# The bidirectional gated scan of a diffusion trunk: units of four tiles, projections by features, and score and output steps for two tiles at once

## The chip, the cores and the metric

The kernel runs on one core of one Trainium2 chip. The metric is device time in microseconds (us) of one execution; lower is better. Shapes are fixed: 2048 latent tokens and 256 context tokens of width 1024, one layer, float32 in and out. Products that must be exact to float32 are made as three TensorE passes over operands that are split into a high and a low part (high x high, high x low, low x high).

## The reference, cut to what matters

```python
def hgrn2_chunk_scan(q, k, v, logf, s0):          # chunks of 64 tokens
    b = jnp.cumsum(logf, axis=3)
    b_ref = b[:, :, :, CHUNK // 2:CHUNK // 2 + 1]
    b_last = b[:, :, :, -1:]
    scores = jnp.einsum('bhnik,bhnjk->bhnij', q * jnp.exp(b - b_ref), k * jnp.exp(b_ref - b))
    o_intra = jnp.einsum('bhnij,bhnjv->bhniv', jnp.where(mask, scores, 0.0), v)
    kv = jnp.einsum('bhnjk,bhnjv->bhnkv', k * jnp.exp(b_last - b), v)
    # S <- exp(b_last) * S + kv over the chunks, s_start = S ahead of each chunk
    o_inter = jnp.einsum('bhnik,bhnkv->bhniv', q * jnp.exp(b), s_start)
    return o_intra + o_inter, s_final

def hgrn2_mixer(h_ctx, h_lat, w_in, lb, g_gain, w_out, need_ctx):
    # w_in (D, 5D): q | f_fwd | f_bwd | i (value) | g (output gate), 8 heads of 128 each
    q = silu(q);  f = lb + (1 - lb) * sigmoid(zf);  logf = log f;  k = 1 - f
    # both directions: scan the context from zero, then the latent tokens from its final state
    o = o_fwd + o_bwd
    return (rmsnorm(o, g_gain) * silu(g)) @ w_out
...
m = silu(c) @ w_ada + b_ada                        # adaLN: shift, scale, gate, twice
lat = lat + g1 * hgrn2_mixer(hc, modulate(rmsnorm(lat), sh1, sc1), ...)
lat = lat + g2 * conv_ffn(modulate(rmsnorm(lat), sh2, sc2), ...)
return rmsnorm(lat, final_g)
```

## The kernel before

Tokens are cut into tiles of 128: tiles -2 and -1 are the context, 0 to 15 the latent tokens. The stages are: adaLN for the first norm (w_ada against the condition, line 209, turned into per-feature A and B, line 224); the scan over heads; the residual stage, which adds the other direction's state (`heads`, line 855), norms, gates, turns (`heads_T`, line 891) and multiplies by the output weight; and the FFN, which the diff doesn't touch.

The scan works in two halves, the groups of `GROUPS`: tiles -2 to 6 and 7 to 15, and in each half through all eight heads, each head in three units of three tiles. The normed, modulated and transposed tokens of a half lie in SBUF as a high and a low part for each unit (`part`, six places). `make_h` prepares a tile: load, square and scale (`normalize`), four transpositions by two into one PSUM buffer (`transpose_mod`, lines 112, 116 and 119), split (lines 80 and 81). The tiles of the second half are prepared inside the last head of the first, between the steps of its units.

A unit (`unit`, line 365) projects with `mm3` (lines 359 to 361: three matmuls for each of eight feature chunks). Gates for the two directions and the query have features as rows and 384 tokens as columns; the value and the output gate have tokens as rows, 256 columns for each tile (`values`, line 413). In the first unit, with two context tiles, query, value and gate of its one latent tile come together with 384 columns and the query is turned; the context values have 256 token columns and are turned. ScalarE takes the sigmoid of the gates (line 405), VectorE their affine `lb + (1 - lb) s` (line 407) and then the factors: running products by `tensor_tensor_scan` (lines 451 and 464), differences and products (`ke`, `qp`, `kd`, `qi`, `km`, `qm`, all three tiles in one instruction); GpSimd makes the small tables `TB` and `TX` and the decays `sd`.

Each tile then has two steps. `part_a` turns `kd` (line 550, copied by ScalarE as `kt`, line 552), makes twelve score matmuls (line 560) and masks them (lines 575 to 577). `part_b` makes `kv` (line 585), `o` from the running state and from the scores (lines 600 and 601), copies both out (lines 602 and 603), updates the state `Sf` on VectorE (line 604) and stores value-sum, `kv`, gate and `qi` in DRAM (`stash`). The steps of one unit are not issued at once; they are a list that the next unit's projections take up by sixths (`fill`) or by chunks (`tick`). TensorE runs what it gets in order, so a step stands between projections, and a wait of a step holds the projections behind it. `ada_rest` (line 631 on) makes the other four adaLN rows with VectorE, one load of 512 KB at a time; `out_weight` multiplies a row block of the output weight by the gate and splits it (lines 653, 80, 81), three for each unit of the last head.

SP issues nearly all loads and stores in order. Weights come through `rawp`, two buffers of 512 KB; at the start 13 buffers take the rows of w_ada and the first head's weights.

The key lines of the order of steps:

```python
order = ((part_a, 0), (part_a, 1), (part_b, 0), (part_a, 2), (part_b, 1), (part_b, 2))
```

Of the kernel before, what the change touches and what calls it, by code (L numbers as in the profile page):

```python
# [38 lines left out]
GROUPS = (  # L39
    ((-2, -1, 0), (1, 2, 3), (4, 5, 6)),  # L40
    ((7, 8, 9), (10, 11, 12), (13, 14, 15)),
)
UN = 384
NSC = 3
NS = 12
# [3 lines left out]
def body(ctx, tc, a, out):  # L49
# [81 lines left out]
    wp = pool_(c1, "wp", 2)  # L131
    hq = pool_(c1, "hq")
    fix = pool_(c1, "fix")


    PLACE = {("h", 0): 0, ("l", 0): 1, ("h", 1): 2, ("l", 1): 3, ("l", 2): 4, ("h", 2): 5}
    parts = {}

    def place(i, shape, dt, name):
        return (hq if i == 5 else hp).tile(shape, dt, name=name, tag=f"place{i}", bufs=1)  # L140

    def part(v, u):

        if (v, u) not in parts:
            parts[v, u] = place(PLACE[v, u], [128, KT, UN], F32R, f"h{v}{u}")
        return parts[v, u]

    def x_tile(p, t, bufs=1, xt=None):
        if xt is None:
            xt = p.tile([128, D], F32, name="xt", tag="xt", bufs=bufs)  # L150
        src, r = (a["x"], t) if t >= 0 else (a["ctx"], t + 2)
        sp.dma_start(xt, src[r * 128:(r + 1) * 128])
        return xt

    def put_split(hm, u, i, ks=slice(None)):

        c = slice(i * 128, (i + 1) * 128)
        split(part("h", u)[:, ks, c], part("l", u)[:, ks, c], hm[:, ks])

    def load_w(h, ty, wh, wl, p=rawp, tag="raw", bufs=2):  # L160
        raw = p.tile([128, D], F32, name="raw", tag=tag, bufs=bufs)
        sp.dma_start(raw, a["w_in"][h, ty])
        split(wh, wl, raw.rearrange("p (k n) -> p k n", k=KT))

    def load_feat(h, **kw):


        feat = []
        for ty in (2, 1):
            wh = wp.tile([128, KT, 128], F32R, name="wh", tag="wh")  # L170
            wl = wp.tile([128, KT, 128], F32R, name="wl", tag="wl")
            load_w(h, ty, wh, wl, **kw)
            feat.append((wh, wl))
        vh = wp.tile([128, KT, 384], F32R, name="vh", tag="vh", bufs=1)
        vl = wp.tile([128, KT, 384], F32R, name="vl", tag="vl", bufs=1)
        load_w(h, 0, vh[:, :, 256:], vl[:, :, 256:], **kw)
        return feat, vh, vl

    def load_vg(h, w, **kw):

        for i in range(2):
            c = slice(i * 128, (i + 1) * 128)
            load_w(h, 3 + i, w[1][:, :, c], w[2][:, :, c], **kw)


    with ExitStack() as c0:
        p0 = pool_(c0, "p0", side="right")
# [5 lines left out]
        staged = [v[:, i] for p, n in ((2, 3), (5, 3), (4, 1))  # L193
                  for v in [place(p, [128, n, D], F32, "x0")] for i in range(n)]

        def early_x(j):

            xt = x_tile(None, first[j], xt=staged[j])
            junk = p0.tile([128, D], F32, name="junk", tag="hm", bufs=3)
            normalize(xt, junk, p0)  # L200

        first = [t for u in GROUPS[0] for t in u]
        for k in range(KT):
            for i in range(2):
                wt = p0.tile([128, D], F32, name="wada", tag="wada", bufs=13)
                (sp if i else act).dma_start(
                    wt, a["w_ada"][k * 128:(k + 1) * 128, i * D:(i + 1) * D])
                for n in range(2):
                    pe.matmul(mps[2 * i + n], silv[:, k, :], wt[:, n * 512:(n + 1) * 512],
                              start=k == 0, stop=k == KT - 1)  # L210
            if 3 <= k < 6:
                early_x(k - 3)
        head0 = load_feat(0, p=p0, tag="wada", bufs=13)
# [12 lines left out]
        hms = [p0.tile([128, KT, 128], F32, name="hm", tag="hm", bufs=3) for _ in range(3)]  # L226
        for g in range(2):
            ks = slice(g * 4, g * 4 + 4)
            for j, hm in enumerate(hms):
                m = 0 if first[j] >= 0 else 1  # L230
                transpose_mod(staged[j], hm, g, p0s, A1[m], B1[m], "tr", 3, (g + j) % 2)
                put_split(hm, 0, j, ks)
        with tc.issue_after(ada_done.ins):
            load_vg(0, head0, p=p0, tag="wada", bufs=13)
        for j in range(3, 7):
            early_x(j)
# [3 lines left out]
        mx = p0.tile([128, 16], F32, name="mx")  # L240
        e2 = p0.tile([128, 2, 16], F32, name="e2")
        eb = p0.tile([128, 32], F32, name="eb")
# [21 lines left out]
    def w_out_part(v, k):  # L264
        if (v, k) not in wos:
            if k < 6:
                keys = [(v, k // 3 * 3 + i) for i in range(3)]
                p = PLACE[v, k // 3]
            else:
                keys = [("h", 6), ("h", 7), ("l", 6)]  # L270
                p = 4
            w = place(p, [128, 3, D], F32R, "wo")
            wos.update({key: w[:, i] for i, key in enumerate(keys)})
        return wos[v, k]


    rest_of_wo = []

    def mixer_scan():
        gp = pool_(c1, "gp", side="right")  # L280
        xp = pool_(c1, "xp", side="right")
# [11 lines left out]
        def mask(name):  # L293
# [1223 lines left out]
```

## Time and profile before

| | us |
|---|---|
| median of three runs (2823.29 to 2826.19) | 2825.01 |
| the profiled execution | 2823.78 |
| its span | 2821.9 |
| first projection of the scan starts | 42.20 |
| last projection of the scan starts | 1283.01 |
| first matmul of the residual stage | 1303.05 |

In the profile's lists PE is TensorE (matmul), PEld its weight load, DVE VectorE, ACT ScalarE, POOL GpSimd, SP SyncE, and L12 is line 12 of the kernel. A timeline row has the start in us, the duration, the engine, the line, the operation, output and inputs by name, the shape and, in brackets, an idle time before it with what ended it; neighbours alike are put in one row with their count. A matmul's duration includes its way through the array, so that matmuls overlap, and the distance from start to start is what one costs in a stream. A row of groups has the count, busy time, mean ns of one, and the idle time before them with what ended it. A row of the waits names who waited for whom: us in total, times, the longest. A row of the windows has the stretch, its length, then the busy time of each engine with the number of instructions, the mean granted clock of TensorE, the share of the DMA engines and GB/s. A row of DMA issues has the count, the size of one and the median us from issue to landing.

### The profile page before, as it was taken

What the parts mean: (1) busy time and instruction counts of PE and PEld (TensorE: products, weight loads), DVE (VectorE), ACT (ScalarE), POOL (GpSimd) and SP (SyncE); (2) the same over time, 40 slices, a digit from 0 to 9 for tenths busy, and PEclk for the clock granted to TensorE, in tenths of its full rate; (3) what the DMA queues carried; (4) which work ended last, traced back from release to release, by engine and by line L of the source; (5) the groups of instructions that cost most, each with busy time, mean ns of one, the idle gap of its engine ahead of it and who ended that gap; (6) DMA issues with size and microseconds to landing.
All of it is one profiled execution on the core that took longest, in us unless ns stands there. A gap on an engine that the chain in (4) does not pass through costs nothing. (4 is left out here: it accounts for less than half of the span.)

```text
span 2821.9 us, 47353 instructions
## 1 busy us (share of the span) xinstructions
PE 2771.7 (98%) x18064; PEld 2443.6 (87%) x18064; DVE 2061.7 (73%) x3619; ACT 1092.2 (39%) x2165; POOL 616.0 (22%) x1019
## 2 busy tenths in 40 slices
PE   8999999999999999998999899999999999999998
PEld 4999999999999999997887688888888888877887
DVE  5766666676766766677997788877877787576887
ACT  5322322354222222233555444444444444333343
POOL 2112222121221211211111443333344331000001
PEclk9999999999999999999999999999999999999999
DMA  6222222222322322236788422226322223987663
GB/s 239 69 84 80 87 84 87 71 93 71 94 86 69 114 72 74 67 96 220 290 308 308 160 90 90 90 69 236 137 82 90 90 88 104 316 296 251 195 197 123
DMA packets 202635, 385.74 MB, mean 137 GB/s; under 512 B 26660, under 2 KB 117796, under 8 KB 197160
## 3 DMA queue, kind: packets, MB, share of 16 engines
q1 hardware_dynamic: 199672, 374.46, 39.2%
q10 hardware_dynamic: 2736, 8.26, 0.8%
q8 instruction: 142, 2.33, 0.3%
q14 instruction: 85, 0.70, 0.1%
HBM read 280.65 MB, written 101.99 MB: 136 GB/s over the span
## 5 line engine op out<-in xcount | busy, mean ns | idle before, releaser
L359 PE MATMUL z<-vh,hh 128*128 128x256 f32 (+1 forms) x1024 | 300.2, 293 | 0.0
L361 PE MATMUL z<-vh,hl 128*128 128x256 f32 (+1 forms) x1024 | 293.2, 286 | 0.0
L360 PE MATMUL z<-vl,hh 128*128 128x256 f32 (+1 forms) x1024 | 293.0, 286 | 0.0
L359 PE MATMUL z<-hh,wh 128*128 128x384 f32 x768 | 264.8, 345 | 3.0 <-ACT hh L80 3.0
L360 PE MATMUL z<-hl,wh 128*128 128x384 f32 x768 | 258.1, 336 | 0.5 <-DVE hl L81 0.5
L361 PE MATMUL z<-hh,wl 128*128 128x384 f32 x768 | 258.2, 336 | 0.0
L1347 PE MATMUL y<-wd,mh 128*128 128x512 f32 x600 | 234.5, 391 | 2.4 <-ACT X L1382 2.1
L1349 PE MATMUL y<-wd,ml 128*128 128x512 f32 x600 | 234.6, 391 | 1.1 <-DVE ml L81 1.1
L1348 PE MATMUL y<-wd,mh 128*128 128x512 f32 x600 | 234.0, 390 | 0.0
L359 PEld LDWEIGHTS z<-vh,hh 128*128 128x128 f32 x1024 | 196.0, 191 | 0.1
L360 PEld LDWEIGHTS z<-vl,hh 128*128 128x128 f32 x1024 | 195.8, 191 | 0.0
L487 POOL COPY TX<-S 128x3 f32<-128x3 f32 x48 | 31.1, 648 | 753.7 <-DVE S L451 753.7
L361 PEld LDWEIGHTS z<-vh,hl 128*128 128x128 f32 x1024 | 195.5, 191 | 0.0
L81 DVE TENSOR_TENSOR w<-raw,w 128x512 fp32r<-128x512 f32 x180 | 142.0, 793 | 45.6 <-ACT w L80 43.6
L80 ACT ACTIVATE w<-raw 128x512 fp32r<-128x512 f32 x180 | 111.9, 629 | 144.1 <-PE zd L752 78.5
L81 DVE TENSOR_TENSOR w<-s,w 128x512 fp32r<-128x512 f32 x126 | 122.1, 974 | 49.6 <-ACT w L80 48.8
L359 PEld LDWEIGHTS z<-hh,wh 128*128 128x128 f32 x768 | 144.8, 189 | 8.8 <-ACT hh L80 3.6
L427 DVE TENSOR_TENSOR st<-z,st 128x128 f32<-128x128 f32 x127 | 36.4, 287 | 153.3 <-ACT st L426 153.1
L360 PEld LDWEIGHTS z<-hl,wh 128*128 128x128 f32 x768 | 145.2, 189 | 0.8 <-DVE hl L81 0.7
L361 PEld LDWEIGHTS z<-hh,wl 128*128 128x128 f32 x768 | 144.8, 189 | 0.0
L422 ACT ACTIVATE v<-z 128x128 f32<-128x128 f32 x128 | 35.4, 277 | 270.6 <-PE z L361 270.5
L749 PE MATMUL zc<-rT,w 128*128 128x512 f32 x352 | 137.1, 389 | 3.1 <-DVE uv L1234 3.0
(327 smaller groups left out, 7840.1 us busy)
## 6 DMA issues: line engine op xcount, KB each, us to landing
raw<-in_w_up_dram SPq DMA_DIRECT2D x88, 512.0 KB, 3.5
raw<-in_w_in_dram SPq DMA_DIRECT2D x80, 512.0 KB, 3.6
lr<-m SPq DMA_DIRECT2D x49, 512.0 KB, 5.8
m<-r SPq DMA_DIRECT2D x66, 256.0 KB, 3.6
raw<-in_w_ada_dram SPq DMA_DIRECT2D x32, 512.0 KB, 4.7
stash<-st SPq DMA_DIRECT2D x125, 128.0 KB, 1.8
kq<-stash SPq DMA_DIRECT2D x15, 1024.0 KB, 7.2
og<-stash SPq DMA_DIRECT2D x15, 1024.0 KB, 6.2
```

What stands on the lines that cost most here:

```text
L80: act.activation(h, src, AF.Copy)
L81: dve.tensor_tensor(l, src, h.bitcast(F32), OP.subtract)
L359: pe.matmul(o, sh[:, k], mh[:, k], start=k == 0, stop=False)
L360: pe.matmul(o, sh[:, k], ml[:, k], start=False, stop=False)
L361: pe.matmul(o, sl[:, k], mh[:, k], start=False, stop=k == KT - 1)
L422: act.activation(v[:, s], z[:, 0:128], AF.Copy)
L427: dve.tensor_tensor(st[:, 1], z[:, 128:256], st[:, 1], OP.mult)
L487: pool.tensor_copy(TX[:, 0, :, 0], tot[:, 0, :, 1])
L749: pe.matmul(o, w[:, 0, k], r[:, :, 0, k], start=start and k == 0, stop=False, skip_group_check=True)
L1347: pe.matmul(z, lh, rh, start=start, stop=False, skip_group_check=True)
L1348: pe.matmul(z, lh, rl, start=False, stop=False, skip_group_check=True)
L1349: pe.matmul(z, ll, rh, start=False, stop=stop, skip_group_check=True)
```

## The change

- The scan has units of four tiles, 512 tokens (`UT`, `NS` = 16). A half is two units, tiles 0 to 7 and 8 to 15; the context tiles are handled apart, in the first half, ahead of the units of each head: gates, factors, values and `context_state`.
- All five projections have features as rows and 512 tokens as columns (`project`, `acc`); the context's have 256. Tokens lie in blocks of one unit and four feature chunks, high and low together (`tok`).
- Values are copied out as `vt`, turned by four transpositions into one PSUM tile and copied as `v` (`values`, `turn`). The output gate stays by features (`swish`, `keep_gate`); in the residual stage it is multiplied after the transposition, and the norm's factor by one VectorE product for four heads and ScalarE copies for the other four.
- The affine of the gates moves from VectorE to ScalarE (`gates`).
- `scores` makes turnings, scores and masks of two tiles at once, `outputs` the `kv` and `o` of two tiles and both updates of `Sf`. Within a pair, the second tile multiplies its scores first and the state last.
- Steps are asked for by a clock of projection triples (`at`, `tick`).
- Weights of one type lie in one tile of four (`wp`). Tiles 8 to 15 are prepared during heads 2 to 5 of the first half, put into DRAM (`tok_d`) and loaded as four blocks of 2048 KB ahead of the second half.
- At the start, w_ada lies in the later token blocks; tiles -2 to 4 are loaded and normed there with the scaling on ScalarE. Output weights 0 to 3 are prepared in the last head, 4 to 7 after it. The split of the residual stage reads SBUF; `pl` (line 1020) takes three places instead of four.

```diff
+        def acc(z, w, rs):
+
+            for k in range(KT):
+                r = rs[k // 4]
+                h, l = r[:, :, 0, k % 4], r[:, :, 1, k % 4]
+                pe.matmul(z, w[:, 0, k], h, start=k == 0, stop=False, skip_group_check=True)
+                pe.matmul(z, w[:, 0, k], l, start=False, stop=False, skip_group_check=True)
+                pe.matmul(z, w[:, 1, k], h, start=False, stop=k == KT - 1, skip_group_check=True)
+                tick()
+        def gates(d, h, u, z):
...
+            act.activation(F, zv[:, :, 31::-1] if d else zv, AF.Sigmoid)
+            act.activation(F, F, AF.Identity, bias=lb[:, j:j + 1], scale=oml[:, j:j + 1])
+        def values(z, n):
+
+            vt = gp.tile([128, UT, 128], F32, name="vt", tag="vt", bufs=1)
+            act.activation(vt[:, 0:n], z, AF.Copy)
+            v = gp.tile([128, UT, 128], F32, name="v", tag="v", bufs=2)
+            def turn():
+                tr = ps.tile([128, n, 128], F32, name="tr", tag="tr")
+                for i in range(n):
+                    pe.transpose(tr[:, i], vt[:, i], ident)
+                act.activation(v[:, 0:n], tr, AF.Copy)
...
+            def outputs(p, v):
...
+                for d in (1, 0):
+                    for i in range(2):
+                        pe.matmul(kv[:, d, i], kt[:, i, d], v[:, s0 + i], start=True, stop=True)
+                for i in range(2):
+                    s = s0 + i
+                    inner = qi[:, 1, 4 * s:4 * s + 4]
+                    pairs = [(inner, Sf[:, h]), (at_[:, i], v[:, s])]
+                    for n, (l, r) in enumerate(pairs[::-1] if i else pairs):
+                        pe.matmul(o[:, i], l, r, start=n == 0, stop=n == 1)
+                    dve.scalar_tensor_tensor(Sf[:, h], Sf[:, h], sd[:, 1, s:s + 1], kv[:, 1, i],
+                                             OP.mult, OP.add)
...
+            gate(0)
+            query(0, (20, 28))
+            gate(1)
+            query(1, (22, 28))
+            value(0, (6, 10))
+            out_gate(0)
+            if g == 1 and h == NH - 1:
+                for k in range(4):
+                    at(clock[0] + 2 * k, lambda k=k: out_weight(k))
+            value(1, (10, 16))
+            out_gate(1)
...
+                if g == 0 and 2 <= h < 6:
+                    for n in range(2):
+                        for i, f in enumerate(make_tok(HT + 2 * (h - 2) + n)):
+                            at(clock[0] + 8 + 44 * n + 8 * i, f)
+                if g == 1 and h == 0:
+                    for u in range(2):
+                        for kh in range(2):
+                            del tok[u, kh]
+                            sp.dma_start(block(u, kh).bitcast(F32), tok_d[u][kh])
...
-            for h in range(NH):
-                dve.scalar_tensor_tensor(og[:, h, 0], og[:, h, 0], rs[:, h:h + 1],
-                                         og[:, h, 1], OP.mult, OP.mult)
+            o = og[:, 0:4, 0]
+            dve.tensor_tensor(o, o, rs[:, 0:4, None].to_broadcast([128, 4, 128]), OP.mult)
+            for h in range(4, NH):
+                act.activation(og[:, h, 0], og[:, h, 0], AF.Copy, scale=rs[:, h:h + 1])
...
-                split(gh[:, hs], gl[:, hs], tp)
+                g = og[:, hs, 1]
+                dve.tensor_tensor(g, tp, g, OP.mult)
+                split(gh[:, hs], gl[:, hs], g)
```

659 lines of the change are left out of this document (311 added, 348 removed).

## The prediction, made before the change was run

> **What bounds the kernel now.** I read the page first: the share of each engine.
>
> ```profile
> PE 2771.7 (98%) x18064; PEld 2443.6 (87%) x18064; DVE 2061.7 (73%) x3619; ACT 1092.2 (39%) x2165; POOL 616.0 (22%) x1019
> ```
>
> TensorE is busy for 98% of the span, so a gain must come out of TensorE's own sequence, and what the change leaves to other engines counts only where it makes TensorE stand still. Next, the windows: the scan, which is nearly all that the diff touches, from its first projection to its last.
>
> ```profile
> 42.00:1283.00 1241.00, 1229.34 (x11033) 1184.19 (x11034) 840.73 (x1858) 395.21 (x1061) 242.55 (x592) 1.00 0.26 82
> ```
>
> After the span of 1241.00 us come the busy times of PE (1229.34), its weight loads, DVE (840.73, 68%), ACT (395.21, 32%) and POOL; the granted clock is 1.00. TensorE is idle for 12 us in all. "Busy" overlaps here, so a matmul's price is its distance to the next one's start. Grouping by line and shape gives the counts, the timeline the distances.
>
> ```profile
> L359 PE MATMUL z<-vh,hh 128*128 128x256 f32 x960 | 278.1, 290 | 0.0
> L359 PE MATMUL z<-hh,wh 128*128 128x384 f32 x768 | 264.8, 345 | 3.0 <-ACT hh L80 3.0
> L359 PE MATMUL z<-hh,vh 128*128 128x384 f32 x320 | 111.2, 347 | 0.0
> ```
>
> ```profile
> 799.75 0.28 PE L360 MATMUL z<-vl,hh 128*128 128x256 f32 x1
> ...
> 804.20 0.28 PE L361 MATMUL z<-vh,hl 128*128 128x256 f32 x1
> 804.32 0.34 PE L359 MATMUL z<-hh,wh 128*128 128x384 f32 x1
> ...
> 808.31 0.34 PE L361 MATMUL z<-hh,wl 128*128 128x384 f32 x1
> 808.49 0.38 PE L550 MATMUL tr<-ident,kd 128*128 128x128 f32 x2
> 808.80 0.32 PE L560 MATMUL sc<-qm,km 128*32 128x64 f32 x8
> 808.93 0.36 PE L560 MATMUL sc<-qp,ke 128*32 128x32 f32 x16
> 809.22 0.44 PE L359 MATMUL z<-hh,wh 128*128 128x384 f32 x1
> 809.50 0.33 PE L360 MATMUL z<-hl,wh 128*128 128x384 f32 x1
> ```
>
> From 799.75 to 804.20 lie 37 steps of 256 columns: 0.1203 us each. From 804.32 to 808.31 lie 23 of 384: 0.1735. The 512-column matmuls of the FFN give the third width, 42 steps in 9.52 us, 0.2267 each:
>
> ```profile
> 1990.11 0.39 PE L749 MATMUL zc<-rT,w 128*128 128x512 f32 x1
> ...
> 1999.63 0.39 PE L749 MATMUL zd<-rB,w 128*128 128x512 f32 x1
> ```
>
> 256 columns more cost 0.1064 us (2.4 columns per ns), and each matmul has a fixed part of about 13.6 ns whatever its width.
>
> **Term 1, wider projections.** Each group above has its like on L360 and L361. Two smaller forms come from the code: in the first unit of eight heads the one latent tile takes 8 x 8 triples of 384 columns, and the context values 8 x 8 triples of 256. That makes 3 x (768 + 320 + 64) = 3456 matmuls of 384 and 3 x (960 + 64) = 3072 of 256, in all 599.6 + 369.6 = 969.2 us. After the change 16 head passes x 2 units x 5 types x 24 = 3840 have 512 columns, and 8 heads x 3 types x 24 = 576 (context) have 256: 870.5 + 69.3 = 939.8 us. The columns stay the same; only 2112 fixed parts go: -29.4 us. Bounds -28 to -30, since all three distances are measured.
>
> The Trainium skill, in "TensorE: Matmul & The Clock Gate", section "Wait — 56ns, not 53.3ns?", has a start-to-start of N / 2.4 GHz plus about 2.5 ns; by that 2112 fewer matmuls would be worth an estimated 5 us. The rows above disagree, with 13 to 14 ns at each of three widths, and they decide the forecast.
>
> **Term 2, values turned afterwards.** Values are now projected by features, so each latent tile needs one transposition per head (128), with 16 for the context as before; the 8 of a query part go. Net 120. A pair of fp32 transpositions took 808.80 - 808.49 = 0.31 us with the change-over, 0.155 each; without one, the kv group below gives 0.44 / 4 = 0.11 for a pass of the same size. They now come four in a row, so the price is 0.11: +13.2 us (upper end +18.6). The ACT copies that go with them (two of 512 columns per unit, 0.6 us) lie on an engine that is 32% busy.
>
> ```profile
> 1266.60 0.61 PE L585 MATMUL kv<-v,kt 128*128 128x128 f32 x4
> 1267.04 0.39 PE L600 MATMUL o<-Sf,qi 128*128 128x128 f32 x2
> ```
>
> **Term 3, scores of two tiles at once.** One tile's group (two turnings, twelve score matmuls) runs from 808.49 to 809.22, 0.73 us, and delays the projection behind it by 809.50 - 809.22 - 0.1735 = 0.11: 0.84 us. What two in a row cost shows at the end of the scan, where the second tile's scores followed at once:
>
> ```profile
> 1283.13 0.38 PE L550 MATMUL tr<-ident,kd 128*128 128x128 f32 x2
> 1283.44 0.32 PE L560 MATMUL sc<-qm,km 128*32 128x64 f32 x8
> ...
> 1284.15 0.49 PE L600 MATMUL o<-Sf,qi 128*128 128x128 f32 x2
> ```
>
> 1.02 us for one pair of turnings and two sets of scores; with the second pair of turnings (0.22) and the 0.11 behind it 1.35, against 2 x 0.84 = 1.68. 64 pairs x 0.33 = -21 us; lower bound half of that, if part of the change-over stays. The number of kv, o and score matmuls does not change. Terms 1 to 3: -37.2 us.
>
> **Term 4, the hand-over inside a pair.** Outputs now run two tiles in one group: the second tile's o<-Sf needs the Sf that DVE updates after the first tile's o<-Sf has read it. In the built order only one to eight projection matmuls stand between, and TensorE takes its work in order, so everything behind waits too. The end of the scan shows this chain without cover:
>
> ```profile
> 1287.76 1.22 DVE L967 TENSOR_TENSOR wo<-raw,wo 128x1024 fp32r<-128x1024 f32 x1
> ...
> 1288.24 0.39 PE L600 MATMUL o<-Sf,qi 128*128 128x128 f32 x2
> ...
> 1289.03 0.35 DVE L604 SCALAR_TENSOR_TENSOR Sf<-Sf,sd,kv 128x128 f32<-128x128 f32 x1
> ...
> 1289.43 0.71 PE L585 MATMUL kv<-v,kt 128*128 128x128 f32 x4 [0.57 <-DVE Sf L604]
> ```
>
> From the read of Sf to the next use: 0.39 + 0.35 and two hops of some 0.06, about 0.85 us with DVE free (here 1.19, as an operation of 1.22 us held DVE until 1288.98). The cover is three o matmuls (0.22 each, that of the read among them) and one projection (0.23), 0.9 us. So the wait is nought with DVE free, and up to about 1.2 us if a long operation has just begun. DVE is 68% busy, mostly with operations of 0.3 to 1.3 us; I take 0.1 us per pair, +6 us, between 0 and +20 (a quarter of the worst, 64 x 1.25 = 80).
>
> **Term 5, the start.** Before, three x tiles were prepared ahead of the adaLN copies; now squares and scaled copies of tiles 1 to 4 also stand ahead of them in ACT's order, and the raw buffers are two instead of thirteen.
>
> ```profile
> 35.73 0.59 ACT L216 ACTIVATE m<-mps 2x512 f32<-2x512 f32 x1 [0.27 <-PE mps L209]
> ...
> 40.48 1.67 ACT L80 ACTIVATE hh<-hm 128x512 fp32r<-128x512 f32 x3
> ...
> 42.20 0.44 PE L359 MATMUL z<-hh,wh 128*128 128x384 f32 x1 [0.71 <-ACT hh L80]
> ...
> 45.83 1.11 ACT L100 ACTIVATE junk<-x 128x1024 f32<-128x1024 f32 x1
> ```
>
> A tile costs ACT about 1.11 (square) + 1.1 (scaled copy, by the same size), so four cost some 8.9 us: last m copy at about 45 instead of 36.3, first projection near 51. Only three context projections (72 x 0.12 = 8.7 us) can then run, and the first unit of 512 needs tiles 0 to 3 split, which go through one hm buffer and one turning buffer at some 5 us each: first latent projection near 73 to 74. Before, stalls of some 7 us lay there too (waits for hh, x, hm). I take +12, between +5 (the tiles overlap) and +16.
>
> **Term 6, the middle.** Today the second half's tiles are prepared inside one head, and TensorE waits there:
>
> ```profile
> PE tp L112 <- ACT kt L552: 1.7, 2, 1.1
> PE tr L550 <- DVE hm L119: 1.4, 1, 1.4
> PE kv L585 <- DVE Sf L593: 1.1, 1, 1.1
> PE kv L585 <- DVE Sf L604: 0.4, 1, 0.4
> ```
>
> These 4.6 us, of a window 595 to 665, go, since the change spreads that work over four heads: -4.6. In their place four blocks come back from DRAM, as transfers of the size of
>
> ```profile
> rT<-rhs0T SPq DMA_DIRECT2D x4, 2048.0 KB, 10.7
> ```
>
> The first two are freed by the output gate of the first half's last unit of tiles 0 to 3, two projections (10.9 us) and their step work ahead of need, some 14 to 16 us with the half projection between the two blocks; behind them on SP nothing is due but the next weights, whose loads stand ahead. Hidden, at a risk of 0 to +5. What hides it are those two projections: without them it costs 10.7.
>
> **Term 7, the end of the scan.** Four output weights are prepared after the last head, the last two loads waiting for raw buffers, and the first stash loads queue behind them on SP.
>
> ```profile
> 1290.42 1.95 PE L869 MATMUL oi<-Sb,kq 128*128 128x128 f32 x16
> 1295.88 0.46 PE L869 MATMUL oi<-Sb,kq 128*128 128x128 f32 x2 [3.50 <-DVE rs L76]
> ...
> 1303.05 0.77 PE L906 MATMUL y<-wo,ghl 128*128 128x512 f32 x1
> ```
>
> From the last projection's end (1283.13) to the first residual matmul pass 19.9 us now, 8 of them idle. Each weight takes DVE 1.28 + 1.22 us, so the raw buffer for the last is free some 5.5 us after the end and the stash of tile 15 lands near +12 instead of before it; I reckon 23.5 us to the residual and 3.4 us less work within: +7, between +3 and +10.
>
> **Edits at nothing.** The gate's affine goes from DVE to ACT; per-unit factors keep their element counts, with a third fewer instructions. Scores are asked for 20 or more ticks of three matmuls (13 us) after the query, against about 8 us of DVE work behind it. In the residual stage DVE loses eight products per tile and gains three wider ones, ACT gains four copies; the stage is TensorE's:
>
> ```profile
> 1400.00:1450.00 50.00, 50.00 (x283) 43.14 (x282) 44.71 (x112) 26.77 (x61) 7.93 (x7) 1.00 0.80 298
> ```
>
> 0, within 3 either way; if TensorE's cover were gone there, DVE's 44.71 of 50 us would be next. The FFN is untouched.
>
> **Sum.** -29.4 + 13.2 - 21 + 6 + 12 - 4.6 + 7 = -16.8 us, against the profiled execution's 2823.78 (span 2821.9 and 1.9 around it): 2807. The median of the runs is 1.2 us above that execution, so 2808.
>
> **Rivals.** (a) Slower: the hand-over in a pair decides. Without it the sum is -22.8; above 0.45 us per pair (64 x 0.45 = 28.8) the kernel is slower by more than 5.6. For it: 1.19 us in the row above with DVE occupied, and a DVE that is 68% busy. Against it: the cover of 0.9 us, and DVE's many short operations. At 1 us per pair: +64 - 22.8 = +41, about 2866. (b) No change that can be measured: the start and the end cost their upper bounds (+7 more), turnings too (+5), and the pairs save half (+10): 2830, or about 2824 with two of the three. (c) A larger gain: the start costs +5, the hand-over and the risks nothing: -30, 2795. (d) The fixed part of a matmul doesn't go: if the weight load sets the distance and grows with a 512-column neighbour, term 1 is -5 and the sum +7.6: 2833. Against it: weight loads are 1184 of 1241 us busy beside the narrow matmuls, and the 512-column row already includes them. This is the case that the skill's 2.5 ns would give.
>
> **How the numbers follow.** A difference of 0.2%, 5.6 us, is about what the measurement can tell from none. The forecast has 0.48, its own range 2796 to 2820; (c) 0.17; (b) 0.16, half of it inside 0.2% and the rest above or below; (a) 0.16; (d) 0.03. So faster 0.65, same 0.15, slower 0.20. The range 2792 to 2838 leaves out the worst of (a) and the best of (c).
>
> **What would show it.** The page after should have 3840 projections of 512 columns about 0.227 us apart and no wait near the start of the second half; the first of them near 73; o<-Sf waits in the list of waits (0.1 us a pair; more speaks for (a)); between the last projection and the first residual matmul about 23 us. I am wrong if the projections stand further apart, if the waits for Sf, at or kd sum to over 25 us, or if the blocks come late.

## The result, and the profile after

The changed kernel takes 2856.1 us in the median (2853.37 to 2858.47, 4 runs) against 2824.47 us before (2823.29 to 2826.19, 4 runs): 1.0111 times as long, 95% interval 1.0094 to 1.0129. It is slower by 32 us where 17 us less was forecast, and lies outside the range. The profiled execution of the changed kernel took 2855.47 us, its span is 2853.8.

First the share of the engines in the changed kernel, from the page:

```profile
PE 2764.3 (97%) x16072; PEld 2277.4 (80%) x16072; DVE 1988.9 (70%) x2900; ACT 1158.9 (41%) x1910; POOL 574.6 (20%) x884
```

TensorE is busy for 7.4 us less, and the span grew by 31.9: the time went into standing still and into slower work, not into more work. To find where, I cut both spans at the same four events: the first projection, the last projection, the first and the last residual matmul. Windows of the kernel before between these events (stretch, length, busy time of PE, PEld, DVE, ACT, POOL with counts, granted clock, share of DMA, GB/s):

```profile
42.20:1283.00 1240.80, 1229.34 (x11033) 1184.19 (x11034) 840.53 (x1858) 395.01 (x1060) 242.55 (x592) 1.00 0.26 81
1283.00:1303.00 20.00, 12.94 (x145) 11.09 (x144) 14.96 (x41) 8.44 (x20) 1.76 (x2) 0.86 0.82 306
1303.00:1531.00 228.00, 227.24 (x1231) 193.90 (x1231) 196.67 (x482) 117.80 (x261) 35.81 (x30) 1.00 0.77 287
```

And of the changed kernel:

```profile
52.60:1284.80 1232.20, 1209.07 (x9114) 1010.82 (x9113) 770.65 (x1216) 428.45 (x729) 196.47 (x452) 0.99 0.30 95
1284.80:1315.00 30.20, 15.89 (x73) 14.06 (x72) 20.45 (x38) 9.36 (x20) 2.08 (x3) 0.66 0.77 275
1315.00:1568.00 253.00, 236.59 (x1231) 196.20 (x1232) 196.44 (x409) 140.91 (x323) 33.82 (x30) 0.98 0.74 260
```

| stage | before | after | difference | forecast |
|---|---|---|---|---|
| to the first projection | 42.2 | 52.6 | +10.5 | +8.9 |
| first to last projection | 1240.8 | 1232.0 | -8.8 | -29.3 |
| last projection to first residual matmul | 20.0 | 30.5 | +10.4 | +3.6 |
| residual stage | 228.5 | 253.0 | +24.5 | 0 |
| the rest (FFN) | 1290.4 | 1285.7 | -4.7 | 0 |

(The exact events lie some tenths beside the edges of the windows; the sum of the differences is 31.9. The scan's forecast is -16.2 for terms 1 and 2, -21 for term 3, +6, -4.6, the 3.1 of the start that lie behind the first projection, and 3.4 of term 7's +7: the prediction reckons 23.5 us, +3.6, for the end itself, and 3.4 us of work that moves out of it.) The residual stage, where nothing was expected, misses by 24.5 us, the scan by 20.5 and the end by 6.8.

**The projections are what was forecast.** Groups and a stretch of the timeline of the changed kernel:

```profile
L332 PE MATMUL z<-tok,w 128*128 128x512 f32 x1280 | 516.7, 404 | 0.1
L332 PE MATMUL z<-cxt,w 128*128 128x256 f32 x192 | 57.0, 297 | 0.0
```

```profile
1167.17 0.39 PE L334 MATMUL z<-tok,w 128*128 128x512 f32 x1
...
1179.86 0.39 PE L333 MATMUL z<-tok,w 128*128 128x512 f32 x1
```

3 x 1280 of 512 columns and 3 x 192 of 256, and 56 steps in 12.69 us: 0.2266 us each.

**Where TensorE stands.** The list of TensorE's waits in the changed kernel (us in total, times, longest):

```profile
PE o L543 <- DVE Sf L544: 12.4, 14, 3.8
PE y L917 <- ACT ghl L77: 10.0, 7, 3.3
PE oi L877 <- DMA kq<-stash: 9.3, 2, 4.8
PE mt L213 <- ACT m L209: 8.1, 1, 8.1
...
PE tr L476 <- ACT vt L470: 2.5, 3, 1.6
```

The first is the hand-over of term 4, the second the residual stage, the third the end of the scan, the fourth the start.

To see all of the scan's loss I added up, over every matmul from the first to the last projection, the distance to the next start, and set against it a clean pace for each kind (0.2267, 0.1735 and 0.1203 us for 512, 384 and 256 columns, 0.112 for a pass of kv or o, 0.109 for a transposition, 0.013 for a score, 0.428 for an adaLN row). What is above the clean pace counts as a wait if it lies over 0.1 us above the median for the same kinds of matmul ahead, here and behind:

| us | before | after | difference |
|---|---|---|---|
| clean pace of all matmuls | 1180.7 | 1165.0 | -15.7 |
| change-overs at scores | 41.7 | 21.0 | -20.7 |
| change-overs at kv and o | 1.6 | 5.2 | +3.6 |
| projections and turnings above their pace | 1.9 | 8.8 | +6.9 |
| waits | 15.1 | 32.2 | +17.1 |

The first row is a count of matmuls times their pace, so its -15.7 (-16.2 forecast) says that the forecast counted rightly; that the pace holds is shown by the 56 steps above. The second row is measured: -20.7, where term 3 has -21. The gain was all there; the waits and the slower pace took 27.6 us of it, of which 4.5 had been forecast.

**One long wait of the hand-over** in the changed kernel's timeline:

```profile
979.93 1.22 DVE L78 TENSOR_TENSOR w<-raw,w 128x1024 fp32r<-128x1024 f32 x1
...
981.14 0.39 PE L543 MATMUL o<-Sf,qi 128*128 128x128 f32 x2
981.17 5.55 SPq L586 DMA_DIRECT2D raw<-in_w_ada_dram  x2
...
985.08 1.28 DVE L590 SCALAR_TENSOR_TENSOR acc<-raw,sil,acc 128x1024 f32<-128x1024 f32 x1 [3.60 <-DMA raw<-in_w_ada_dram]
986.28 0.34 DVE L544 SCALAR_TENSOR_TENSOR Sf<-Sf,sd,kv 128x128 f32<-128x128 f32 x1
986.67 0.80 PE L543 MATMUL o<-Sf,qi 128*128 128x128 f32 x2 [3.78 <-DVE Sf L544]
```

The state could have been updated at 981.6. But VectorE's next instruction was an adaLN row product that stood 3.60 us for a 512-KB load. Only behind it came the update, and TensorE stood 3.78 us. The load was late because it, too, had waited for VectorE: weights and adaLN rows share the two buffers of `rawp`, and the load was issued at 981.17, when VectorE's split of a weight (L78 at 979.93, the last reader of a `raw` buffer) had just ended. The loads behind VectorE's waits of 3.62 us (until 696.47) and 3.53 us (until 1126.86) were issued right behind such a split as well; no run gives the rows a buffer of their own. The two passes behind the wait took 0.80 us instead of 0.39, and a window around the place shows a lower clock:

```profile
980.00:990.00 10.00, 6.22 (x29) 5.06 (x28) 4.22 (x8) 1.36 (x3) 0.00 (x0) 0.83 0.40 122
```

The granted clock is 0.83 there. The Trainium skill, "TensorE: Matmul & The Clock Gate", section "HAM oscillation — how this bites in real kernels", asks for no idle of TensorE above about 3.4 us; this row, with a wait of 3.78 us, agrees. Shorter waits were not safe here, though: behind two of 2.46 and 1.55 us in the residual stage (until 1376.65 and 1381.04) the clock of the window 1380:1385 was 0.73.

**The residual stage.** Two neighbouring tiles in the changed kernel's timeline: the split of the first ends and the next load into its buffer is issued; the second is turned, multiplied by its gate, split and used (the rows of other work are left out):

```profile
1412.77 0.69 DVE L78 TENSOR_TENSOR ghl<-og,ghl 128x512 fp32r<-128x512 f32 x1
...
1413.52 0.32 SPq L858 DMA_DIRECT2D og<-stash  x1
...
1417.47 1.04 PE L906 MATMUL tp<-ident,og 128*128 128x128 f32 x8
...
1420.44 1.28 DVE L881 TENSOR_TENSOR og<-og,oi 128x512 f32<-128x512 f32 x2 [1.54 <-DMA og<-stash]
...
1423.44 0.68 DVE L908 TENSOR_TENSOR og<-tp,og 128x512 f32<-128x512 f32 x1
...
1424.15 0.63 ACT L77 ACTIVATE ghl<-og 128x512 fp32r<-128x512 f32 x1 [1.73 <-DVE og L908]
...
1426.41 0.48 PE L917 MATMUL y<-wo,ghl 128*128 128x512 f32 x1
```

The transposition ends near 1418.5, yet its product with the gate (L908) starts only at 1423.44: ahead of it in VectorE's order stand the add of the next tile (L881), which waits 1.54 us for its load, and the work behind that add. That load could be issued only when the tile before had freed the buffer. The product alone doesn't free it: its result is written back into the buffer and the split reads it there. The split's last operation (L78) ends at 1413.46, the load is issued at 1413.52; all 14 loads behind the first two are issued within 0.1 us of that operation's end, 1.4 to 3.8 us after the product's. VectorE's waits for this load, of the kernel before (its residual stage) and of the changed one:

```profile
DVE og L873 <- DMA og<-stash: 1.4, 2, 1.1
```

```profile
DVE og L881 <- DMA og<-stash: 17.0, 8, 3.7
```

In this tile TensorE still had other passes until 1426.4. Its waits in the stage, before (1304 to 1520 us) and after (1316 to 1550):

```profile
PE y L908 <- DVE ghl L81: 0.3, 1, 0.3
```

```profile
PE y L917 <- ACT ghl L77: 9.3, 6, 3.3
PE tp L109 <- DVE rs L73: 2.8, 3, 1.8
PE tp L109 <- DVE xn L929: 2.8, 2, 2.5
PE y L919 <- DVE ghl L78: 0.8, 2, 0.6
```

That is 15.7 us instead of 0.3. In the windows above TensorE is also busy for 9.4 us more with the same matmuls (236.59 against 227.24), at a granted clock of 0.98 instead of 1.00; together that is about the 24.5.

So the theory for the residual stage: the gate product and the split that reads it come after the transposition and so keep the tile's buffer (two in all) longer, the next load lands late, VectorE stands before the add, and the product behind it is late too: a loop through a buffer, a queue and an in-order engine. The rival: one VectorE operation more on the way from transposition to matmul.

**The end of the scan** in the changed kernel:

```profile
1290.29 0.80 PE L543 MATMUL o<-Sf,qi 128*128 128x128 f32 x2 [3.72 <-DVE Sf L544]
...
1294.49 0.33 SPq L858 DMA_DIRECT2D kq<-stash  x1
...
1300.57 3.60 PE L877 MATMUL oi<-Sb,kq 128*128 128x128 f32 x16 [4.79 <-DMA kq<-stash]
```

The stash load of the last tile is issued 9.9 us after the last projection (1284.62; in the kernel before 2.5 us ahead of it, at 1280.52). The 16 passes that wait for it start 16.0 us after the last projection and take 3.60 us where they took 1.95 before.

**The start** in the changed kernel:

```profile
41.76 1.15 ACT L100 ACTIVATE x<-x,rs 128x1024 f32<-128x1024 f32 x1 [0.91 <-POOL rs L74]
42.81 2.00 ACT L209 ACTIVATE m<-mps 2x512 f32<-2x512 f32 x4
...
52.65 0.56 PE L332 MATMUL z<-cxt,w 128*128 128x256 f32 x1
...
74.83 0.78 PE L332 MATMUL z<-tok,w 128*128 128x512 f32 x1
```

The adaLN copies end at 44.8 (45 forecast), behind the last scaled copy; the first projection is at 52.65 (51) and the first latent one at 74.83 (73 to 74).

### The profile page after: what moved, and what is told of

Same layout as the page of the kernel before. It is cut to its first block, busy times and chain, and to the rows that moved or that the text cites. A ratio compares the mean times of both kernels' runs of the same rounds, so it can differ in the third digit from the quotient of the medians.

```text
span 2853.8 us, 41978 instructions
## 1 busy us (share of the span) xinstructions
PE 2764.3 (97%) x16072; PEld 2277.4 (80%) x16072; DVE 1988.9 (70%) x2900; ACT 1158.9 (41%) x1910; POOL 574.6 (20%) x884
## 4 chain that ended last, share of the span: by engine, by line
PE 71%; DMA 11%; DVE 11%; ACT 3%; issue 2%; POOL 2%; SPq 0%; DVEq 0%; POOLq 0%; ACTq 0%
PE z L332 9%; PE z L334 9%; PE z L333 9%; PE y L1359 3%; PE y L1357 3%; PE y L1358 3%; PE zd L759 3%; PE zc L759 3%; PE zc L761 3%; PE zd L761 3%; PE zd L762 3%; PE zc L762 3%; PE za L761 3%; PE za L762 3%; PE za L759 3%
## 5 line engine op out<-in xcount | busy, mean ns | idle before, releaser
L332 PE MATMUL z<-tok,w 128*128 128x512 f32 x1280 | 516.7, 404 | 0.1
L333 PE MATMUL z<-tok,w 128*128 128x512 f32 x1280 | 505.1, 395 | 0.0
L334 PE MATMUL z<-tok,w 128*128 128x512 f32 x1280 | 501.8, 392 | 0.3 <-DVE w L78 0.3
L78 DVE TENSOR_TENSOR w<-raw,w 128x512 fp32r<-128x512 f32 (+1 forms) x260 | 239.3, 924 | 88.3 <-ACT w L77 86.1
L332 PEld LDWEIGHTS z<-tok,w 128*128 128x128 f32 x1280 | 241.3, 189 | 49.7 <-issue 2.6
L334 PEld LDWEIGHTS z<-tok,w 128*128 128x128 f32 x1280 | 240.9, 188 | 50.0 <-DVE w L78 0.6
L333 PEld LDWEIGHTS z<-tok,w 128*128 128x128 f32 x1280 | 241.6, 189 | 44.3
L77 ACT ACTIVATE w<-raw 128x512 fp32r<-128x512 f32 (+1 forms) x260 | 195.9, 760 | 177.4 <-PE zd L762 77.4
L78 DVE TENSOR_TENSOR w<-s,w 128x512 fp32r<-128x512 f32 x126 | 121.2, 967 | 53.9 <-ACT w L77 53.1
L759 PE MATMUL zc<-rT,w 128*128 128x512 f32 x352 | 137.1, 390 | 1.2 <-DVE uv L1244 1.0
L762 PE MATMUL zc<-rT,w 128*128 128x512 f32 x352 | 137.0, 389 | 0.0
L761 PE MATMUL zc<-rT,w 128*128 128x512 f32 x352 | 136.9, 389 | 0.0
L1357 PEld LDWEIGHTS y<-wd,mh 128*128 128x128 f32 x600 | 113.3, 189 | 27.2 <-ACT X L1392 3.7
L385 DVE TENSOR_TENSOR_SCAN S<-F,d 128x528 f32<-128x528 f32 (+1 forms) x80 | 91.5, 1144 | 62.2 <-ACT F L368 62.1
L77 ACT ACTIVATE w<-s 128x512 fp32r<-128x512 f32 x126 | 78.2, 627 | 138.8 <-POOL s L815 81.8
L1359 PEld LDWEIGHTS y<-wd,ml 128*128 128x128 f32 x600 | 113.2, 189 | 25.3 <-DVE ml L78 1.4
L1358 PEld LDWEIGHTS y<-wd,mh 128*128 128x128 f32 x600 | 113.3, 189 | 23.4
L759 PE MATMUL za<-rB,w 128*128 128x512 f32 x336 | 130.7, 389 | 0.0
L761 PE MATMUL za<-rB,w 128*128 128x512 f32 x336 | 130.7, 389 | 0.0
```

What stands on the lines that cost most here:

```text
L77: act.activation(h, src, AF.Copy)
L78: dve.tensor_tensor(l, src, h.bitcast(F32), OP.subtract)
L332: pe.matmul(z, w[:, 0, k], h, start=k == 0, stop=False, skip_group_check=True)
L333: pe.matmul(z, w[:, 0, k], l, start=False, stop=False, skip_group_check=True)
L334: pe.matmul(z, w[:, 1, k], h, start=False, stop=k == KT - 1, skip_group_check=True)
L385: dve.tensor_tensor_scan(flat(S[:, d]), flat(F[:, d]), flat(d1[:, 0:ns]), 0.0, OP.mult, OP.max)
```

## The experiments

All times are medians beside the kernel before on the same chip. That kernel took 2824.5 us beside the changed one and 2822.9, 2823.2 and 2825.2 us beside the others, so a gain is given as the difference of what each lies above it; the change lies 31.6 us above. Three edits first, each aimed at one stage, and with the first of them one run that leaves work out and one that makes the stage's edit alone.

**Two loads for value-sum and gate.**

```diff
-    ogs2 = qp.tile([128, 2, NH, 2, 128], ...)
+    ogs2 = qp.tile([128, 2, 2, NH, 128], ...)
...
                 gts[t - 3] = load_stash(1, t - 3)
+            if t > 1:
+                gates2[t - 2] = load_stash(2, t - 2)
```

> The changed kernel with one thing other: value-sum and output gate of a tile come by two loads into two buffers, the gate's asked for a period later, so that the next value-sum no longer waits until the gate has been multiplied. Theory A (the residual stage lost its 24.5 us because a tile's buffer is held until the late gate product, so that the next load lands late and VectorE, in order, stands before the add): VectorE's wait for that load falls from 17.0 us to under 4, TensorE's wait for the split (9.3 us) nearly goes, and the stage from first to last residual matmul goes from 253.0 to 228 to 236 us; total 2832 to 2840. Rival B (the one VectorE product more between transposition and matmul is the cost, wherever the load stands): the stage stays above 246 us and the total within 6 us of 2856.

Measured: 2829.07 us, ratio 1.002 (1.0011 to 1.003), 6.1 us above the kernel before and so 25.5 less than the change. The residual stage of this kernel as a window, and VectorE's wait for the load:

```profile
1313.40:1542.00 228.60, 227.63 (x1231) 193.67 (x1232) 196.06 (x411) 139.49 (x321) 34.58 (x30) 1.00 0.82 289
```

```profile
DVE og L886 <- DMA og<-stash: 0.6, 1, 0.6
```

The stage is 228.7 us long instead of 253.0, the wait 0.6 us instead of 17.0, with every operation of the changed stage still in its place. Theory A holds; the operation by itself isn't the cost. (The total is 3 us under the expected band.) The two loads are also half as large, but they land hardly sooner: 5.9 us after their issue in the median, against 6.4.

**No gate product.** Here the product with the output gate is left out.

```diff
-                g = og[:, hs, 1]
-                dve.tensor_tensor(g, tp, g, OP.mult)
-                split(gh[:, hs], gl[:, hs], g)
+                split(gh[:, hs], gl[:, hs], tp)
```

> The changed kernel without the product with the output gate: the split reads the transposition's PSUM directly as before the change; the gate is stored and loaded but left out of the result. Both theories expect the stage back near 228 to 232 us (total 2830 to 2836), A since the buffer is free at the transposition, B since the chain is one operation shorter. If it stays above 240 us, neither holds and the split of the norm's factor between VectorE and ScalarE or the loads themselves are the cause.

Measured: 2824.74 us (ratio 1.0007, 0.9998 to 1.0017; 5 us under the expected band), the stage 227.0 us. Value-sum and gate come by one load here, as in the change, so the size of the load alone isn't the cause either: the split reads the turned tile directly, the buffer is free at the transposition again, and VectorE's wait for the load is gone from its list. What the product costs in the stage when the loads are apart is 228.7 - 227.0 = 1.7 us; the medians of the two runs lie 4.3 us apart. No run separates the product from the split's reading of the buffer.

**The same edit alone, on the kernel before.** The other direction:

```diff
-            for h in range(NH):
-                dve.scalar_tensor_tensor(og[:, h, 0], og[:, h, 0], rs[:, h:h + 1],
-                                         og[:, h, 1], OP.mult, OP.mult)
+            o = og[:, 0:4, 0]
+            dve.tensor_tensor(o, o, rs[:, 0:4, None].to_broadcast([128, 4, 128]), OP.mult)
+            for h in range(4, NH):
+                act.activation(og[:, h, 0], og[:, h, 0], AF.Copy, scale=rs[:, h:h + 1])
...
-                split(gh[:, hs], gl[:, hs], tp)
+                g = og[:, hs, 1]
+                dve.tensor_tensor(g, tp, g, OP.mult)
+                split(gh[:, hs], gl[:, hs], g)
```

> The kernel before with only the residual stage's edit: the norm's factor by one VectorE product for four heads and four ScalarE copies, and the output gate multiplied after the transposition; the gate is stored there by tokens, so the product takes it unturned. Theory A (the held buffer makes the stage long, by itself and without any of the scan's edits): the stage from first to last residual matmul goes from 228.5 to 245 to 255 us, VectorE waits over 12 us for the load of the value-sum, total 2840 to 2850. Rival: the stage stays under 235 us here, and the loss needs something else of the change, such as the stash written in smaller pieces or the end of the scan coming later.

Measured: 2848.55 us, ratio 1.0083 (1.0067 to 1.0099). Window of the stage and VectorE's wait in this kernel:

```profile
1303.00:1558.00 255.00, 237.14 (x1233) 196.98 (x1232) 195.39 (x409) 139.69 (x321) 33.43 (x30) 0.97 0.74 259
```

```profile
DVE og L873 <- DMA og<-stash: 19.7, 10, 4.2
```

The stage goes from 228.5 to 255.2 us, 0.2 over the band. It is the edit of the residual stage, alone, whatever the scan does before it: 23.4 us in the total.

**Outputs of a pair in two steps.**

```diff
-                for i in range(2):
+                def tile_out(i):
...
+                tile_out(0)
+                at(clock[0] + 2, second)        # second: tile_out(1), copies and stores
```

> The changed kernel with the outputs of a pair in two steps, the second tile two projection triples (1.36 us) behind the first; scores stay in pairs. Theory C (TensorE stands in the scan because the second tile's use of the state follows the first within 0.9 us): the waits of o for Sf up to the last projection fall from 8.7 us to under 3 us, the last projection starts 6 to 10 us earlier (1275 to 1279 us instead of 1284.6). Rival D (the waits come from VectorE standing before an operation that waits for a transfer, so 1.36 us more are too few for the long ones): the short ones of some 0.3 us in the first half go (2.6 us), the long ones of the second half (up to 3.8 us) stay, and the last projection starts 2 to 5 us earlier, the rest of the change being switches between steps and projections.

Measured: 2841.11 us, ratio 1.0065 (1.005 to 1.008), 13.5 us less than the change. The last projection starts at 1275.1, and of the waits for the state there is left:

```profile
PE o L543 <- DVE Sf L544: 3.7, 3, 1.9
```

That is in the whole kernel, and none of it before the last projection: the long waits of o went too, against rival D. Time alone isn't the reason, as this run's timeline shows at the place of the long wait:

```profile
978.14 0.35 DVE L544 SCALAR_TENSOR_TENSOR Sf<-Sf,sd,kv 128x128 f32<-128x128 f32 x1 [0.65 <-PE o L543]
...
981.01 1.28 DVE L595 SCALAR_TENSOR_TENSOR acc<-raw,sil,acc 128x1024 f32<-128x1024 f32 x1 [2.52 <-DMA raw<-in_w_ada_dram]
```

VectorE still stands for the load, but the first tile's update now comes ahead of that product in its order, and only the second tile's, which is needed a group later, behind it. A part of the wait comes back there: kv waits 1.47 us for ScalarE's copy at 983.02. By the accounting above the scan's waits behind the first 150 us fell from 19.2 to 11.1 us and the change-overs at kv and o from 5.2 to 2.0. In the profiled executions 9.6 us lie in the scan and some 3 behind it.

**Norming of tiles 1 to 4 behind the adaLN copies.**

```diff
-        for t in range(1, 5):
-            early_x(t)
+        with tc.issue_after(ada_done.ins):
+            for t in range(1, 5):
+                early_x(t)
```

> The changed kernel with the loading and norming of x tiles 1 to 4 asked for only behind the adaLN copies, as the diff left it to the scheduler before. Theory E (ScalarE's squares and scaled copies ahead of the adaLN copies delay the whole scan): the first projection starts at 43 to 46 us instead of 52.7, but the tiles are needed soon after, so the first latent projection only 2 to 6 us earlier than 74.8; total 2 to 6 us less. Rival F (the four tiles' preparation sets the first latent projection, in whatever order): it starts at 74 to 78 us and the total is the same within 2 us.

Measured: 2849.03 us, ratio 1.0092 (1.0076 to 1.0109), 5.5 us less than the change. First projection and first latent projection of this kernel:

```profile
40.65 0.39 PE L333 MATMUL z<-cxt,w 128*128 128x256 f32 x1 [0.26 <-ACT cxt L77]
```

```profile
69.33 0.77 PE L333 MATMUL z<-tok,w 128*128 128x512 f32 x1
```

The first projection is 12 us earlier (a little earlier than expected), the first latent one 5.5. E holds, and F doesn't: the first latent projection is at 69.33, not at 74 to 78. That the four tiles' preparation sets what is left is likely, since TensorE's waits until then are those of their transpositions and of the context (14.4 us in all, the longest 4.1), but wasn't tried.

**All three together.**

> The two loads, the outputs in two steps and the later norming of tiles 1 to 4 together, on the changed kernel. Theory G (the three losses lie in different stages and add): 2856 - 27 - 15 - 7 gives 2807, with a range of 2803 to 2814: first latent projection near 69, last projection near 1269, stage 228 to 230 us; clearly faster than the kernel before (2823). Rival H (the shares overlap or the clock takes them back): above 2818.

Measured: 2815.33 us (2812.57 to 2819.78, 9 runs), ratio 0.9971 (0.9962 to 0.9981): faster than the kernel before. It lies 7.9 us below the kernel before, so the three edits give 39.5 us of the 44.5 that their sum makes; the last projection starts at 1271.6 (1269 expected), the stage takes 229.3. The total lies between what G expects (up to 2814) and what H expects (above 2818); 5 us are not accounted for.

**Scores of a pair in two steps**, on top of all three.

```diff
-                kts[p] = turned(kd, 2 * p, 2)
...
+                tile_scores(0)
+                if h == 0 and t0 == 0:
+                    second()
+                else:
+                    at(clock[0] + 2, second)    # second: tile_scores(1), copy, masks
```

> As the kernel with all three, but turnings and scores of a pair in two steps, the second tile's two triples behind the first's (in the first head at once), and one copy and one masking for the pair as before. Theory K (term 3: each group pays its change-over, 0.33 us): 63 pairs make the last projection 18 to 22 us later and the total 15 to 22 us longer than with all three. Rival L (the change-over is hidden or was paid already by the row of steps): less than 8 us longer.

Measured: 2840.66 us, ratio 1.006 (1.0047 to 1.0074), 25.3 more than with all three; the last projection at 1295.6 instead of 1271.6. The scan as a window, with all three edits and then with scores in two steps besides:

```profile
41.50:1271.60 1230.10, 1205.96 (x9112) 1010.91 (x9113) 773.15 (x1223) 435.23 (x741) 204.58 (x456) 0.99 0.31 95
```

```profile
41.30:1295.60 1254.30, 1227.17 (x9111) 1015.81 (x9112) 776.66 (x1225) 433.19 (x741) 206.93 (x456) 0.99 0.30 93
```

As many matmuls, 21.2 us more busy time and a scan that is 24.2 us longer: change-overs at scores rise from 20.7 to 41.3 us by the accounting, 0.33 us for each of 63 pairs. Term 3 is shown, slightly above its band.

**Early last outputs, and two buffers for the last weights.** Two attempts at the end of the scan, on top of all three.

```diff
-            value(1, (10, 16))
+            value(1, (4, 8) if g == 1 and h == NH - 1 else (10, 16))
```

> As the kernel with all three, and in the last head of all the outputs of the last unit are asked for 4 and 8 triples behind the value instead of 10 and 16, so that most of them lie under the last projection. Theory I (the end of the scan is long because the last outputs and their stores come only then, and the first stash load waits for their buffers): from the last projection to the first residual matmul 22 to 26 us instead of 29 to 30, total 3 to 7 us less than with all three. Rival J (VectorE's four output weights and the weight loads ahead on SP set the end): the same within 2 us.

Measured: 2813.08 us (2812.39 to 2816.19, 5 runs), the end 25.6 us long instead of 28.7. The end moved as theory I says, but the total by 2.3 us, within the spread of both kernels.

```diff
-            raw = rawp.tile([128, D], F32, name="raw", tag="raw")
+            p, tag = {6: (xp, "hm"), 7: (xp, "stg")}.get(k, (rawp, "raw"))
+            raw = p.tile([128, D], F32, name="raw", tag=tag)
```

> As the kernel with the early outputs, and the last two output weights (6 and 7) are loaded into two buffers of their own that are idle in the second half, so that they don't wait for the buffers of weights 4 and 5 and the first stash load isn't queued behind them on SP. Theory I expects no more than 2 us against the early outputs alone; J expects the stash load of tile 15 issued some 3 to 6 us earlier and 3 to 6 us less in total.

Measured: 2811.74 us (2810.29 to 2818.77, 5 runs), ratio to the kernel before 0.9964 (0.9951 to 0.9977), the end 24.2 us. The load of tile 15 is issued at 1278.04 instead of 1281.10, 5.8 us after the last projection, as J expects, but the total falls by 1.3 us, as I does, again within the spread; so neither is shown. TensorE waits for the load all the same, and its clock falls meanwhile:

```profile
1272.20:1296.40 24.20, 11.69 (x58) 10.70 (x57) 15.42 (x28) 7.35 (x18) 2.94 (x3) 0.65 0.81 288
```

What holds that load besides the weights isn't settled; ahead of it on SP stand the stores of the last output gate.

**Values turned two triples later**, on top of the last.

```diff
-                at(clock[0] + 2, turn)
+                at(clock[0] + 4, turn)
...
-            value(1, (4, 8) if g == 1 and h == NH - 1 else (10, 16))
+            value(1, (6, 9) if g == 1 and h == NH - 1 else (10, 16))
```

> As the kernel with the early outputs and the two buffers for the last weights, and the transpositions of the values are asked for four triples behind the projection instead of two (the last outputs at 6 and 9). Theory M (what is left of the scan's idle, some 5 us before the turning of values, comes from ScalarE's copy not being done 1.36 us after the projection): the waits of the turning for the copy go from 4 us to under 1 us and the total is 2 to 5 us less than 2812. Rival: the copy stands behind a split that waits for a weight's transfer, longer than 2.7 us; then less than 1 us is gained.

Measured: 2816.81 us (2812.07 to 2819.7, 6 runs), ratio 0.997 (0.9958 to 0.9982): no gain. The waits of this kernel:

```profile
PE kv L543 <- ACT sk L559: 6.4, 3, 2.7
...
PE o L549 <- DVE Sf L550: 6.0, 3, 3.7
...
PE tr L482 <- ACT vt L476: 1.1, 2, 0.7
```

The turning's wait went from 4.1 to 1.1 us and came back one step on: kv's wait for ScalarE's copies from 3.4 to 6.4. The state's went from 1.5 to 6.0, but 5.0 of it lies behind the last projection, where this run also moves the outputs. It is ScalarE and VectorE that are late at such places, and a later step only meets them elsewhere, which fits the rival. In the run before this one ScalarE stood 4.69 and 4.29 us for a weight's load (until 752.88 and 966.03) just ahead of the two copies that the turning waited for. In this one kv's longest wait, until 979.73, goes back by ScalarE's copy and the update of the state to an adaLN product that stood 3.13 us for its load. A run without these loads wasn't made.

## Why the prediction was wrong, point by point

- **Terms 1 and 2** (wider projections, values turned): right, by the counts and the pace: 0.2266 us a projection, -15.7 us against -16.2. So the fixed part of a matmul went, against rival (d).
- **Term 3** (scores in pairs): right, -20.7 against -21 in the accounting, and +24 us when undone alone.
- **Term 4** (hand-over): the mechanism was right, the size was not. The forecast let VectorE be held by a long operation of up to 1.25 us and took 0.1 us a pair, +6. 14 waits made 12.4 us, 8.7 of them in the scan. The first nine, up to 760 us, are of the size that was forecast, at most 0.4 us each and 2.6 together; eight of them stand behind an operation of 0.4 to 0.7 us. The four behind them make 6.1 us: there VectorE had itself stood for a load shortly before, 3.60 us in the row shown and 3.1 to 3.5 at the others, and the granted clock around the longest was 0.83. The last, 3.7 us at the end of the scan, lies behind the work on the output weights. Undone, the scan is 9.6 us shorter and the kernel 13.5. It was not rival (a) either, which had 64 pairs wait and 2866 us: hardly a quarter of them did.
- **Term 5** (start): +10.5 to the first projection against +8.9, and some 3 us behind it; the order on ScalarE was the cause for the first projection, and of 5.5 us of the total.
- **Term 6** (middle): the 4.6 us went, and the reloaded blocks made no wait in the list. But new waits came in other places: the row products of the adaLN, now all in the second half, hold VectorE; the turning of values waits 2.5 us for ScalarE.
- **Term 7** (end): +10.4 where 23.5 us, +3.6, was reckoned for this stage. The stash was expected near +12 and came at +16.0. By the windows TensorE's idle time went from 7.1 us (the prediction reads 8) to 14.3, with 9.3 us of waits for the stash and 3.7 for the state. Its busy time went from 12.9 to 15.9 us with half as many matmuls, at a granted clock of 0.66 against 0.86; the first 16 passes took 3.60 us instead of 1.95. What holds the load is not settled.
- **Edits at nothing**: this is the step that failed most, 24.5 of the 48.7 us between forecast and result (31.9 and 16.8). The residual stage was costed by busy time: VectorE loses and gains about as much, ScalarE has room, TensorE covers all. Busy time was right (DVE 196.67 and 196.44 us). What it can't show is how long a buffer is held. Before, a tile's buffer was free at the transposition; after, at the end of the split that reads the product, behind VectorE's queue. The load, the add, the product, the split and the next load formed a loop, and a tile took 15.8 us instead of TensorE's 14.3.
- **Rival (b)** had start and end at their upper bounds, dearer turnings and pairs that save half, 2824 to 2830; the start and the end did come near their bounds, but the pairs saved all, and the slowness came from places without a rival.

The FFN part became 4.7 us shorter without an edit. In the lists of TensorE's waits those of `zc` and `zd`, which lie there, are 12.8 us before and 10.0 after; the cause is open.

## What to carry to other kernels

When a read of a loaded buffer is moved behind another step, follow the buffer: who frees it now, which load waits for that, and which in-order engine stands before that load; here a stage lost 24 us with VectorE's busy time unchanged, and giving the late operand a buffer and a load of its own brought it back. A wait behind an in-order engine is priced not by that engine's longest operation (1.28 us in the row shown) but by the longest time that an operation ahead of it stands for a transfer (3.60 us). And parts of a change can be worth more than the whole: with its losses removed, this one is 0.29% to 0.36% faster than the kernel before.

## What the runs showed of the hardware

A stop of TensorE cost more than its length here: the windows shown that hold waits of 3.7 to 7.2 us have a mean granted clock of 0.65 to 0.83, and behind such a wait passes of the same shape took about twice as long (0.80 us for two instead of 0.39).
